# Retention's output projection by seven block products in two phases of two heads, its residual turned by VectorE and its partial sums kept in DRAM

## The chip, the cores and the metric

The kernel runs on one core of a Trainium2 chip. Its time is the device time of one execution in microseconds (us), and the median of several executions is what is compared. The engines of the core are TensorE (PE in the profile; PEld is its loading of weights), VectorE (DVE), ScalarE (ACT), GpSimd (POOL) and SyncE (SP), which here issues most DMAs. Each engine works through its own queue in order.

## The reference

A trunk of two layers on a prompt of 1024 tokens and on 8 single decode tokens, in fp32, with 1024 features. Layer 0 is retention (4 heads, key width 256, value width 512), layer 1 is attention over a sliding window.

```
h = rmsnorm(x, g_norm)
q, k, v, gate = split(h @ w_in)                    # 1024 -> 1024, 1024, 2048, 2048
o, S = retention_scan(q, k, v, S0)                 # in chunks of 128 tokens, head by head
o = rmsnorm(o, g_out) per head                     # over a head's 512 values
o = o * silu(gate)
return x + o @ w_out, S                            # 2048 -> 1024: the projection that changes
```

Layer 1 norms the result, projects it to q, k, v and a gate, attends, and has an output projection and a residual of its own.

## The kernel before

Every fp32 number of a product is split into a high part and a low part (names ending in `_hi`/`h` and `_lo`/`l`), and each product is three matmuls: high by high, low by high, high by low. ACT writes a high part as a copy in PE's format; DVE or POOL subtracts it from the number for the low part.

**Stage 1, retention's input projection (0 to about 532 us).** Mostly by seven block products: tokens are split into even and odd ones, the features in two halves and the output columns in two blocks, so that the product of 2 x 2 by 2 x 2 blocks takes seven block products (table `SEQ7`, L309) of sums of blocks, not eight. The sums of the token side stand in cells (`XH`, `XL`, in two token halves t); those of the weights (S1 to S4) are made set by set. `product` (L312) issues a block product for one token half: 12 matmuls of 128x258 (256 prompt columns and 2 decode columns). `evac` (L361) adds the banks up in SBUF. The order of all other engines is set by a table of planned times: a function is put behind a slot of PE (`later`) or at a planned microsecond (`when`). Gates go through Silu and are stored in DRAM (`gsc`).

**Stage 2, the retention loop (about 532 to 681 us).** 32 steps, a head's chunk each: heads 0 and 1 in turns, then heads 2 and 3. A step has scores and products on PE (`b_qk`, `b_mm`), and behind them the sum of squares (ACT, L987), its power on POOL (L116), the scaling `on` (DVE, L999), a turn by transposes on PE (`b_tr`), and the gated output `og` = turned output x gate (DVE, L1011). Then `b_oh` (ACT, L1018) and `b_ol` (POOL, L1022) split `og` into `A_hi`, `A_lo` (tokens 0 to 511) or `B_hi`, `B_lo` (the rest and the decode tokens). `others(i)` writes each step's operations in a fixed order for every engine.

**Stage 3, the output projection (681 to 878 us).** Plain: for each of 8 blocks of 128 output columns and three groups of tokens (512, 256, 264) 16 contraction tiles x 3 matmuls go into one PSUM bank (`ro_part`, L1214 to L1216). The first of these tiles is woven into the loop's last steps (`b_wmm`, L1055 to L1057). Weights are loaded on SP's queue in tiles of 512 KB and multiplied by the output norm's gain while they are split (L1147, L1148). The residual x_prompt is added by PE: it is transposed into the same bank (`tr`, L101). `ro_finish` copies the sum out (ACT, `x`), splits it times the next norm's gain into `A_hi`, `A_lo` (L1252, L1253), squares it (L1258), adds the squares on POOL (L1259) and stores it to `xscr`; the first token group is read back and split later (`reload2`, L1267, L1268).

**Stage 4** begins with the key and value projection (`kv_mm`, L1387 to L1389), which needs all of `A_hi` and `A_lo`.

## Time and profile before

| | |
|---|---|
| median of 3 runs | 1313.93 us (1312.88 to 1314.59) |
| the profiled execution's own time, its span | 1313.03 us, 1310.9 us |
| PE, DVE, ACT, POOL busy | 98%, 56%, 53%, 48% of the span |
| granted TensorE clock | 0.997 |
| DMA | 193.98 MB, 148 GB/s on average |

A row of a view by stage has the stretch, its length, then for each engine the busy time and the number of instructions, the granted clock, the mean busy share of the 16 DMA engines and the rate. A row of a group has the line, engine and operation, what it writes and reads, the shape, the count, and behind the bars the busy time, the mean duration in ns and the engine's idle time ahead of it, with what ended that. Matmuls are pipelined, so their durations overlap; a matmul's price is the distance between two starts.

### The profile page before, as it was taken

To read this page: it belongs to the slowest core of one execution; us is meant where nothing else is said; L and a number is where in the kernel's file an instruction comes from. 1 tells how busy PE (TensorE), PEld (TensorE's weight loads), DVE (VectorE), ACT (ScalarE), POOL (GpSimd) and SP (SyncE) were. 2 spreads that over 40 slices of the span, in tenths; PEclk is the share of its full clock that TensorE was granted. 3 is DMA by queue.
4 is the path that set the end of the run, shared out by engine and by line. 5 is a ranking of instruction groups with operands and counts; after the bars stand their busy time and mean duration, and the time that the engine had idled before them with its cause. 6 is when DMAs were issued, how large, how long until landed. Compare 5 with 4: busy or idle time off the path is not lost.

```text
span 1310.9 us, 26102 instructions
## 1 busy us (share of the span) xinstructions
PE 1280.8 (98%) x9597; PEld 1208.3 (92%) x9597; DVE 728.0 (56%) x1476; ACT 691.5 (53%) x1722; POOL 630.9 (48%) x800
## 2 busy tenths in 40 slices
PE   6999999999999999999999999999999999999998
PEld 5999999999999999887886889999998999998998
DVE  6944556566565564587784333324565666766321
ACT  5533544554555653577775444445576666666121
POOL 6654534545445544599970110127476676554000
PEclk9999999999999999999999999999999999999999
DMA  6314767677686854456556553452032111237232
GB/s 228 102 61 133 235 200 243 181 234 220 195 241 184 249 172 138 134 177 216 169 163 186 161 166 121 131 147 85 17 100 79 66 59 43 74 109 252 73 96 78
DMA packets 199907, 193.98 MB, mean 148 GB/s; under 512 B 12916, under 2 KB 180140, under 8 KB 199764
## 3 DMA queue, kind: packets, MB, share of 16 engines
q1 hardware_dynamic: 165024, 157.78, 39.4%
q10 hardware_dynamic: 34756, 34.53, 8.3%
q8 instruction: 76, 1.25, 0.4%
q14 instruction: 51, 0.42, 0.1%
HBM read 132.23 MB, written 61.08 MB: 147 GB/s over the span
## 4 chain that ended last, share of the span: by engine, by line
PE 89%; POOL 3%; DVE 2%; DMA 2%; ACT 2%; issue 1%; ACTq 0%; SPq 0%; POOLq 0%; DVEq 0%
PE b L331 7%; PE b L332 7%; PE b L333 7%; PE pj L1167 6%; PE pj L1168 6%; PE pj L1169 6%; PE b L324 4%; PE b L325 4%; PE b L326 4%; PE tr L101 4%; PE pj L1214 4%; PE pj L1216 4%; PE pj L1215 4%; PE o L1645 2%; PE b L538 2%; DMA wr<-in_w_out_ret_dram 1%
## 5 line engine op out<-in xcount | busy, mean ns | idle before, releaser
L331 PE MATMUL b<-xh,woh 128*128 128x258 f32 x784 | 223.2, 285 | 0.0
L333 PE MATMUL b<-xh,wol 128*128 128x258 f32 x784 | 221.7, 283 | 0.0
L332 PE MATMUL b<-xl,woh 128*128 128x258 f32 x784 | 221.6, 283 | 0.0
L1167 PE MATMUL pj<-A_hi,wh 128*128 128x384 f32 (+1 forms) x512 | 174.5, 341 | 2.0 <-ACT A_hi L1665 1.3
L1168 PE MATMUL pj<-A_lo,wh 128*128 128x384 f32 (+1 forms) x512 | 164.7, 322 | 0.2 <-DVE A_lo L1666 0.2
L1169 PE MATMUL pj<-A_hi,wl 128*128 128x384 f32 (+1 forms) x512 | 164.6, 321 | 0.0
L331 PEld LDWEIGHTS b<-xh,woh 128*128 128x128 f32 x784 | 148.0, 189 | 4.1 <-issue 3.7
L332 PEld LDWEIGHTS b<-xl,woh 128*128 128x128 f32 x784 | 148.7, 190 | 0.0
L333 PEld LDWEIGHTS b<-xh,wol 128*128 128x128 f32 x784 | 148.0, 189 | 0.0
L222 POOL TENSOR_TENSOR wol<-raw,woh 128x512 fp32r<-128x512 f32 x52 | 68.1, 1319 | 130.3 <-ACT woh L217 126.2
L324 PE MATMUL b<-woh,xh 128*128 128x256 f32 x448 | 126.6, 283 | 0.0
L325 PE MATMUL b<-wol,xh 128*128 128x256 f32 x448 | 126.0, 281 | 0.0
L326 PE MATMUL b<-woh,xl 128*128 128x256 f32 x448 | 125.6, 280 | 0.0
L1167 PEld LDWEIGHTS pj<-A_hi,wh 128*128 128x128 f32 x512 | 96.8, 189 | 6.0 <-issue 2.6
L1168 PEld LDWEIGHTS pj<-A_lo,wh 128*128 128x128 f32 x512 | 97.1, 190 | 0.4 <-DVE A_lo L1666 0.4
L1169 PEld LDWEIGHTS pj<-A_hi,wl 128*128 128x128 f32 x512 | 96.5, 188 | 0.0
L1148 DVE SCALAR_TENSOR_TENSOR wl<-wr,gcol,wh 128x256 fp32r<-128x256 f32 x128 | 53.9, 487 | 69.9 <-ACT wh L1147 65.8
L1259 POOL TENSOR_TENSOR acc<-acc,sq 128x256 f32<-128x256 f32 (+1 forms) x28 | 20.6, 743 | 148.1 <-ACT sq L1258 148.0
L1625 POOL TENSOR_TENSOR s<-s,sm 128x512 f32<-128x512 f32 x64 | 66.5, 1040 | 47.6 <-DVE sm L1624 43.5
L324 PEld LDWEIGHTS b<-woh,xh 128*128 128x128 f32 x448 | 84.3, 188 | 5.0 <-issue 2.9
L326 PEld LDWEIGHTS b<-woh,xl 128*128 128x128 f32 x448 | 84.3, 188 | 0.0
L325 PEld LDWEIGHTS b<-wol,xh 128*128 128x128 f32 x448 | 84.3, 188 | 0.0
(391 smaller groups left out, 3631.4 us busy)
## 6 DMA issues: line engine op xcount, KB each, us to landing
raw<-in_w_in_ret_dram ACTq DMA_DIRECT2D x44, 512.0 KB
st<-in_state_ret_dram SPq DMA_DIRECT2D x64, 256.0 KB
out_dram<-st SPq DMA_DIRECT2D x64, 256.0 KB
wr<-in_w_out_ret_dram SPq DMA_DIRECT2D x32, 512.0 KB
wr<-in_w_in_swa_dram SPq DMA_DIRECT2D x18, 512.0 KB
vb<-vscr SPq DMA_DIRECT2D x64, 128.0 KB
evp<-qks SPq DMA_DIRECT2D x32, 256.0 KB
evx<-vsc SPq DMA_DIRECT2D x32, 256.0 KB
```

Of the source, the lines that this page charges most:

```text
L222: eng.tensor_tensor(lo, src_of(s, name, sub), hi.bitcast(F32), SUB)
L324: mm(dst, xh, wh, start=a and i == 0, stop=False, skip_group_check=True)
L325: mm(dst, xh, wl, start=False, stop=False, skip_group_check=True)
L326: mm(dst, xl, wh, start=False, stop=z, skip_group_check=True)
L331: mm(dst, wh, xh, start=a, stop=False, **sg)
L332: mm(dst, wh, xl, start=False, stop=False, **sg)
L333: mm(dst, wl, xh, start=False, stop=z, **sg)
L1148: nc.vector.scalar_tensor_tensor(lo[:, k, :], raw[:, k % 4, :], gk, hi.bitcast(F32)[:, k, :], ALU.mult, ALU.subtract)
L1167: mm(ps, hi[:, k, fs], xh[:, k, t0:t1], start=first and k == ks[0], stop=False)
L1168: mm(ps, hi[:, k, fs], xl[:, k, t0:t1], start=False, stop=False)
L1169: mm(ps, lo[:, k, fs], xh[:, k, t0:t1], start=False, stop=last and k == ks[-1])
L1625: nc.gpsimd.tensor_tensor(st[:, :, 0:256], st[:, :, 0:256], sm.unsqueeze(2).broadcast_to([128, 2, 256]), ALU.mult)
```

## The change

Stage 3 is done by stage 1's seven block products. The contraction of 2048 rows is split in two phases: phase 0 has heads 0 and 1, phase 1 heads 2 and 3. Each phase has four sets, one for 256 output columns each; a set's blocks are even and odd tokens, the two heads of the phase, and even and odd output columns. Seven of the eight sets have 7 products x 2 token halves of 12 matmuls 128x258; set 4, the first of phase 1, is computed plainly (8 slots of 24), without sums.

- **Loop.** `on` goes from DVE to ACT; `b_oh` and `b_ol` go away. `og` is stored by a DMA on SP's queue: heads 0 and 1 into cells in SBUF, heads 2 and 3 into DRAM (`osc`). `x_items` makes the token side's sums and splits for phase 0 in the loop, 3 or 4 items a step. The first set's weights are loaded and split there too (`p_early`).
- **Gates.** The output norm's gain is multiplied into the gates in stage 1 (POOL, 64 times 128x258) and no more into the weights.
- **Residual.** `p_xr` loads x_prompt in runs of 64 numbers into one buffer `xr`, half of the tokens at a time; `p_xt` turns it on DVE by 32x32 block transposes (four of 128x256 for a half) into the tiles to which the products are added.
- **Partial sums.** Phase 0's results are stored to DRAM (`pscr`) on ACT's queue and loaded again in phase 1 in place of the residual.
- **Cells of phase 1.** In sets 3 to 5 the gated outputs of heads 2 and 3 are loaded from `osc`, summed and split (`split`, `t_sums`).
- **End.** `p_fin` squares and stores the results; in set 7 it splits them for the next stage, and the six other blocks are read back and split by `a_load` and `a_split`. The key and value projection's weights are loaded and split in set 7. The layout of `xscr` and the order of layer 1's features (even and odd) follow.

```diff
         if s.kind == "g":
             dst, col = gsc, (s.kt + i) % 4
+            pool.tensor_scalar(r[:, 0:258], r[:, 0:258], gcol[:, s.kt + i:s.kt + i + 1], None, MUL)
...
     def b_on(h, c):
         d = heads[h]
-        dve.tensor_scalar(d["on", c], d.pop(("po", c)), d["ss", c], None, MUL)
+        act(d["on", c], d.pop(("po", c)), AF.Copy, scale=d["ss", c])
...
+        o_ = ogt[h % 2]
+        dve.tensor_tensor(o_, d.pop(("pt", c)).rearrange("p (i t) -> p i t", i=4), d["g", c], MUL)
+        nc.sync.dma_start(out=(osc[h - 2, par, t] if h >= 2 else raw_of(((B11, T1), (B21, B22))[h][par], t))[:, :, cs], in_=o_)
...
+        def parts(x, src):
+            n = len(its)
+            do(act, XH[t][x][:, :, cs], src, AF.Copy)
+            do(lambda: (pool if n % 3 else dve).tensor_tensor(XL[t][x][:, :, cs], src, XH[t][x].bitcast(F32)[:, :, cs], SUB))
...
+    def p_bank(i, t):
+        if i < 2:
+            return sSp.tile([128, DV], F32, tag="S", bufs=4, name="S")
+        return pq["b2"].tile([128, 512], F32, tag=f"b2{t}", name="b2")
...
+    def p_evac(s, j, t):
...
+        if j == 0:
+            act(c["p"][:, t], b0, AF.Copy)
+        elif j == 1:
+            dve.tensor_tensor(c["p"][:, t], b1, c["p"][:, t], ADD)
+        elif j == 2:
+            dve.tensor_tensor(c["x"][:, t], b2, c["p"][:, t], ADD)
+        else:
+            key, b = (("c", b0), ("w", b1), ("x", b2), ("p", b1))[j - 3]
+            dve.tensor_tensor(c[key][:, t], b, c[key][:, t], ADD)
...
+    def p_store(s, key):
+        nc.scalar.dma_start(out=pscr[s.a, "cwxp".index(key)].rearrange("p (t n) -> p t n", t=2), in_=s.c[key])
...
+    def p_xr(s, t):
+        v = x_prompt[0, 512 * t:512 * t + 512, 256 * s.a:256 * s.a + 256].rearrange("(n j) (b f) -> b j n f", j=32, b=4)
+        for b in range(4):
+            nc.sync.dma_start(out=pq["xr"][32 * b:32 * b + 32], in_=v[b])
+
+    def p_xt(s, t):
...
+            dve.transpose(o_.rearrange("p (c y) -> p c y", c=2), v[:, par, i])
...
+    def p_fin(s, key, t):
...
+        if s.n == 7:
+            act(toks(A_hi[:, ft], t, par), x1, AF.Copy, scale=gk)
+            dve.scalar_tensor_tensor(toks(A_lo[:, ft], t, par), x1, gk, toks(A_hif[:, ft], t, par), MUL, SUB)
...
+    def t_sums(t, h):
...
+        dve.tensor_tensor(y, hv(raw_of(T1, t), h), b11, SUB)
+        dve.tensor_tensor(z, hv(raw_of(T2, t), h), y, SUB)
+        part(T1, t, h, y, dve)
+        part(T2, t, h, z, pool)
+        dve.tensor_tensor(b11, z, b11, SUB)
+        pool.tensor_tensor(b21, b21, z, SUB)
...
+    def a_split(k):
+        gk = gcol[:, 16 + k:17 + k]
+        lo_ = A_lo[:, k, 0:NP]
+        act(A_hi[:, k, 0:NP], lo_.bitcast(F32), AF.Copy, scale=gk)
+        dve.scalar_tensor_tensor(lo_, lo_.bitcast(F32), gk, A_hif[:, k, 0:NP], MUL, SUB)
...
+            if s.n:
+                for j in range(2):
+                    when(max(s.t0 - 22.0, 1.5) + 0.1 * j, p_raw, s, j)
+            if s.P == 0:
+                a = s.t0 - 9.0 if s.n else 0.5
+                b = s.t0 - 3.0 if s.n else 5.0
+                when(a, p_xr, s, 0)
+                when(b, p_xt, s, 0)
+                when(b + 0.1, p_xr, s, 1)
+                when(b + 5.5, p_xt, s, 1)
+            else:
+                for key in "cwxp":
+                    when(s.t0 - 7.0, p_part, s, key)
...
+            L(n + 13, o_load, raw_of(T1, t)[:, :, 0:256], 0, 1, t)
+            L(m, o_load, raw_of(T2, t)[:, :, 0:256], 1, 1, t)
...
+            for h in range(2):
+                L(m + 2 + 2 * t + h, t_sums, t, h)
...
+        for k in range(6):
+            L(u + 1 + k, a_load, k)
+            L(u + 4 + k, a_split, k)
```

**The loop, on ACT.** This is one step of the loop before (`Sh`: state split, `on,bss`: sum of squares, `vh`, `kh`, `sTh`: splits of values, keys and scores).

```order
L968 ACTIVATE Sh<-S 128x512 x2
L987 ACTIVATE on,bss<-po 128x512
L795 ACTIVATE vh<-evx 128x512
L1018 ACTIVATE B_hi<-og 128x4x128
L770 ACTIVATE kh<-tr,M_85 128x256
L785 ACTIVATE sTh<-sT 128x128
```

And one of the changed kernel's, with an item of `x_items` (L1078).

```order
L1011 ACTIVATE Sh<-S 128x512 x2
L808 ACTIVATE vh<-evx 128x512
L783 ACTIVATE kh<-tr,M_88 128x256
L1042 ACTIVATE on<-po,bss 128x512
L798 ACTIVATE sTh<-sT 128x128
L1078 ACTIVATE SB<-G_7435 128x4x128
L1030 ACTIVATE on,bss<-po 128x512
```

The split of the gated output (L1018) is gone; the scaling `on` (L1042), which reads POOL's `bss`, stands ahead of the split of the scores.

**The turn, on SP.** The changed kernel's queue at the end of the loop: `osc` are the gated outputs, `xr` the residual, `rb` and `ra` weights.

```order
L1056 DMA osc<-og 512x1x128
L747 DMA evw<-gsc 128x512
L1056 DMA osc<-og 512x1x128 x4
L1215 DMA xr<-in_x_prompt_dram 32x16x64 x4
L1131 DMA rb<-in_w_out_ret_dram 128x4x256 x2
L1215 DMA xr<-in_x_prompt_dram 32x16x64 x12
```

The first residual loads stand behind the last steps' stores.

**Set 0, on DVE.** The changed kernel's queue from the last gated output on (`S` and `b` are PSUM banks, `evp`, `evx`, `evc`, `evw` the tiles in which a set is added up, `rx` and `rp` further residual tiles, `w` low parts of weights).

```order
L1055 TENSOR_TENSOR og<-tr,evw 128x512
L1190 TENSOR_TENSOR evp<-S,evp 128x258
L1229 STREAM_TRANSPOSE evw<-xr 128x256
L1229 STREAM_TRANSPOSE evc<-xr 128x256
L1229 STREAM_TRANSPOSE rx<-xr 128x256
L1229 STREAM_TRANSPOSE rp<-xr 128x256
...
L1195 TENSOR_TENSOR evc<-S,evc 128x258
L1229 STREAM_TRANSPOSE evw<-xr 128x256
...
L1229 STREAM_TRANSPOSE rp<-xr 128x256
L1195 TENSOR_TENSOR evc<-S,evc 128x258
```

Evacuations of PSUM banks (L1190, L1195) stand behind turns of the residual, which wait for its loads; before, DVE had only splits of weights and results in this stage.

680 lines of the change are left out of this document (454 added, 226 removed).

## The prediction

> **What bounds the kernel now.** I read the page first, then the busy times by stage, then the stage's groups, PE's waits and the chain.
>
> ```profile
> PE 1280.8 (98%) x9597; PEld 1208.3 (92%) x9597; DVE 728.0 (56%) x1476; ACT 691.5 (53%) x1722; POOL 630.9 (48%) x800
> PE 89%; POOL 3%; DVE 2%; DMA 2%; ACT 2%; issue 1%; ACTq 0%; SPq 0%; POOLq 0%; DVEq 0%
> ...
> core 0: us, PE busy (x) PEld busy (x) DVE busy (x) ACT busy (x) POOL busy (x), PEclk, DMA share, GB/s
> 340.00:505.00 165.00, 165.00 (x1390) 161.18 (x1389) 98.41 (x174) 89.74 (x204) 73.83 (x96) 1.00 0.69 204
> 618.00:672.00 54.00, 54.00 (x297) 45.86 (x296) 42.37 (x97) 38.59 (x92) 49.60 (x59) 1.00 0.55 175
> 700.00:718.00 18.00, 15.97 (x66) 11.31 (x66) 9.07 (x21) 11.39 (x30) 1.43 (x2) 1.00 0.77 234
> 718.00:798.00 80.00, 80.00 (x435) 68.31 (x435) 25.79 (x62) 35.09 (x92) 8.74 (x12) 1.00 0.46 143
> ```
>
> PE is busy 98% of the span and makes 89% of the chain, at full granted clock. In the output projection (718 to 798) the three other engines are at 11 to 44%, so a product less there is time less, until the new work fills them. In the loop ahead of it (618 to 672) POOL is at 92% and DVE at 78%: little room. The projection runs from its first product to the first of the key and value projection:
>
> ```profile
> 681.47 0.47 PE L1055 MATMUL S<-A_hi,woh 128*128 128x512 f32 x1
> 877.71 0.36 PE L1387 MATMUL pj<-wh,A_hi 128*128 128x256 f32 x1
> ...
> L1214 PE MATMUL pj<-A_hi,wh 128*128 128x512 f32 x112 | 45.1, 403 | 2.4 <-ACT wh L1147 2.4
> L1214 PE MATMUL pj<-B_hi,wh 128*128 128x264 f32 x128 | 37.0, 289 | 0.0
> L1214 PE MATMUL pj<-B_hi,wh 128*128 128x256 f32 x128 | 36.8, 287 | 0.0
> L101 PE MATMUL pj<-ident,xr 128*128 128x128 f32 x60 | 10.7, 280 | 0.0
> ```
>
> That is 196.2 us. The durations in groups overlap (pipelined), so a product's price is read from start to start:
>
> ```profile
> 734.09 0.39 PE L1214 MATMUL pj<-A_hi,wh 128*128 128x512 f32 x1
> 739.84 0.40 PE L1215 MATMUL pj<-A_lo,wh 128*128 128x512 f32 x1
> ...
> 479.89 0.28 PE L331 MATMUL b<-xh,woh 128*128 128x258 f32 x1
> 492.75 0.28 PE L333 MATMUL b<-xh,wol 128*128 128x258 f32 x1
> ```
>
> 25 steps in 5.75 us make 0.230 us for 512 columns; 107 steps in 12.86 us make 0.1202 us for 258 columns, the first stage's form and the one that the change uses.
>
> **What goes from PE.** The new stage has seven sets of 7 products x 2 token halves x 12 matmuls and one plain set of 8 x 24, 1368 matmuls of 258 columns: 164.4 us. A slot of 12 is 1.44 us, a set 20.2, the plain one 23.1. Gain: 196.2 - 164.4 = 31.8 us. The residual's PE transposes and PE's 2.4 us of waits on weights are inside the 196.2. Everything below is what eats into it.
>
> ```profile
> L222 DVE TENSOR_TENSOR wol<-s,woh 128x512 fp32r<-128x512 f32 x88 | 67.5, 770 | 11.1 <-ACT woh L217 11.0
> L376 DVE TENSOR_TENSOR evp<-b,evp 128x258 f32<-128x258 f32 x26 | 11.1, 426 | 13.3 <-PE b L333 13.3
> L999 DVE TENSOR_SCALAR on<-po,bss 128x512 f32<-128x512 f32 x31 | 23.3, 750 | 14.0 <-POOL bss L116 14.0
> L1022 POOL TENSOR_TENSOR A_lo<-og,A_hi 128x512 fp32r<-128x512 f32 x16 | 20.7, 1292 | 0.0
> L1018 ACT ACTIVATE A_hi<-og 128x512 fp32r<-128x512 f32 x16 | 10.2, 637 | 0.4 <-DVE og L1011 0.4
> L1589 POOL TENSOR_SCALAR ndp<-C 128x256 f32<-128x256 f32 x16 | 13.7, 854 | 13.8 <-DVE s L1613 12.8
> ```
>
> **Gates in the first stage.** 64 new scalings on POOL x 0.854 = 55 us, by the row of 256 columns. From 340 to 505 POOL has 91 of 165 us free, and what waits behind a scaling is one store and the release of its buffer. Lower bound 0, upper 5 (should one POOL burst hold a set's buffers); I take 1.0.
>
> **The loop.** Over 32 steps POOL loses b_ol (32 x 1.29 = 41 us) and gains 18 low parts (23 us). ACT loses b_oh (20 us), gains `on` (32 x about 0.6) and 28 high parts (18 us). DVE loses `on` (24 us) and gains 16 sums and 10 low parts at 0.77 (20 us) with 14 pairs of decode columns. So the totals nearly cancel; the order does not. The 14.0 us that DVE waited for POOL's power go over to ACT, where the score split sTh and the state split Sh stand behind `on`, and PE's next products wait for both. ACT had 15.4 of 54 us free. Each og also becomes a DMA on SP's queue, ahead of the next steps' q, k, v and gate loads; those are issued two steps ahead, which covers it. POOL, the fullest engine, gets lighter, so a gain of 2 us is possible; the other bound is +10 (most of the 14 us exposed). I take +2.5.
>
> **The turn.**
>
> ```profile
> 684.82 0.75 DVE L999 TENSOR_SCALAR on<-po,bss 128x512 f32<-128x512 f32 x1 [0.72 <-POOL bss L116]
> 687.75 0.69 DVE L1011 TENSOR_TENSOR og<-tr,evw 128x512 f32<-128x512 f32 x1 [0.47 <-PE tr L101]
> ...
> 674.36 3.05 DMA evx<-in_w_out_ret_dram
> 704.42 5.29 DMA wr<-in_w_out_ret_dram
> 697.60 4.54 DMA wr<-in_w_out_ret_dram
> ...
> 797.32 0.37 SPq L1226 DMA_DIRECT2D xr<-in_x_prompt_dram  x1
> L806 DVE CAST qh<-evp 128x256 fp32r<-128x256 f32 x28 | 9.6, 341 | 0.0
> ```
>
> The last norm ended 4.1 us after the stage's first product. In the new order its turn on PE stands behind two slots (2.9 us): PE waits 1.2 us (0 to 3). Then come the turn (0.6) and og (0.7), so the last og is ready 5.4 us after the stage's first product, and only behind its store, on SP's queue, stand the four residual loads of set 0's first token half.
>
> **Set 0's residual.** One half is 512 KB in 2048 runs of 256 bytes. 256 KB in 512-byte runs landed in 3.05 us, 512 KB in 1 KB runs in 4.54: 1.56 fixed and 1.49 for each 512 runs of 512 bytes. By bytes a half lands in 4.5 us; if a run of 256 bytes is as dear as one of 512, in 1.56 + 4 x 1.49 = 7.5, and with four issues of 0.37 in 9.0. I take 5.5, near the bytes, since the queues are otherwise nearly empty at that point. Four turns of 128x256 on DVE cost 1.4 (the cast of that size) to 3.1 (0.77 each); I take 1.6. There is one landing buffer: the second half's loads wait for the first half's turns. So the second half is turned at 5.4 + 2 x 7.1 = 19.6, and behind it in DVE's queue stands the evacuation of the fourth product's second half (0.4), which frees the PSUM bank that the ninth slot after the first, at 9 x 1.44 = 13.0, writes. PE waits 7.0 us; bounds 17.6 - 13.0 = 4.6 and 30.0 - 13.0 = 17.0.
>
> The Trainium skill (DMA: Bandwidth & Descriptors, Specifications) speaks against these loads: under 512 bytes a transfer does a read-modify-write and falls from line rate. No run here shows such loads; by it a half lies at its upper bound, 9.0, and the sum comes out as in the slower rival.
>
> The later sets of phase 0 start their first half 9 us ahead. A cycle of two halves is 14.2 of 20.2 us, covered by the set before; stores of the partial sums run on ACT's queue. I take 1.0; with 12.1 a half, 3 x (24.2 - 20.2) = 12.
>
> **Sets 3 to 5, where the cells are made again.** Twelve reloads of 512 KB of gated outputs, 1 MB of partial sums and 1 MB of weights: 8 MB, at the 234 GB/s of 700 to 718 some 36 us, where set 3 and the plain set last 43.3. The last sums need T2, which lands last, and behind it DVE does four times two sums, a low part and one more sum (4 x 4 x 0.77 = 12.3), evacuations (8 x 0.43), two more low parts, decode columns and the low part of set 5's first operand, in all about 27 us in the plain set's 23.1. Counted by DVE alone set 5 starts 4 us late; counted from the landing of T2, with half of the sums behind it and the rest of the queue, 36 + 12.3 + 10 - 43.3 = 15. I take 7.0: T1 lands earlier, so part of the sums is done by then. Set 6: 0.5 (0 to 2).
>
> **Set 7 and the tail.**
>
> ```profile
> L1268 DVE SCALAR_TENSOR_TENSOR A_lo<-wr,gcol,A_hi 128x512 fp32r<-128x512 f32 x8 | 6.0, 752 | 9.8 <-ACT A_hi L1267 9.8
> L1267 ACT ACTIVATE A_hi<-wr,gcol 128x512 fp32r<-128x512 f32 x8 | 5.8, 722 | 7.9 <-DMA wr<-xscr 7.9
> L1253 DVE SCALAR_TENSOR_TENSOR A_lo<-pj,gcol,A_hi 128x256 fp32r<-128x256 f32 x8 | 3.9, 483 | 24.1 <-ACT A_hi L1252 23.8
> L1252 ACT ACTIVATE A_hi<-pj,gcol 128x256 fp32r<-128x256 f32 x8 | 3.7, 467 | 0.0
> L1258 ACT ACTIVATE sq<-x 128x256 f32<-128x256 f32 x21 | 8.5, 413 | 0.3
> ```
>
> In the last ten slots (14.4 us) ACT has six splits of 1024 columns (6 x 1.44) and eight A_hi and squares (8 x 0.88): 15.7 us; DVE has 6 x 1.50 + 8 x 0.48 + 8 x 0.43 and the decode columns, about 17.5. Before, nearly all of that lay under PE. The next projection needs every A_lo: 3 us late, and the last evacuation, split and square follow the last product. I take 4.0 (2 to 8).
>
> **Costed at nothing.** The norm gains' new order (two transposes on PE early in the first stage), the decode columns' small stores, and the next projections' weights loaded in pairs of rows (runs of 1 KB as before) lie under DMA engines that are half idle here; a weight load without that cover would cost its landing, up to 5.3 us.
>
> **The sum.** 1.0 + 2.5 + 1.2 + 7.0 + 1.0 + 7.0 + 0.5 + 4.0 = 24.2 against 31.8: 7.6 us less than the profiled execution's 1313.0, so 1305.4. The median of the runs is 0.9 above that execution: 1306.
>
> **The rivals.** (1) The bounds' lower ends hold: -2 + 4.6 + 4 + 2 = 8.6 of losses, 1291. For it: other engines at 11 to 44% in this stage. Against it: single buffers and in-order queues. 0.18. (2) ACT paces the loop: its new wait for POOL's power is exposed, +10 in place of +2.5, 1314, no change. For it: those 14.0 us, and that PE is never idle there now. Against it: 28% of ACT is free. 0.14. (3) Slower: the residual's loads pace phase 0. If loading and turning a half costs 12.1 us in place of 7.1, set 0 loses 17 and each later set of the phase 4: 21 us more than in the sum, 1327. From 10.1 us a half (half of a set) it decides every set. For it: 256-byte runs that no row shows, one buffer, and DVE's queue in which evacuations stand behind the turns. (The Trainium skill's rule named above would act through this rival.) Against it: DMA engines at half load. With sets 3 to 5 near 15, lesser cases of it also end slower. 0.25. My forecast has 0.43, with 1300 to 1312 as its own range.
>
> What differs by under 0.2% (2.6 us) cannot be told from no change. Of my 0.43 some 0.03 falls there, with rival 2 it is 0.17; faster 0.40 + 0.18 = 0.58; slower 0.25. The range 1291 to 1324 reaches to rivals 1 and 3.
>
> **What would show it.** Products at 0.120 us and set 1 in 20 to 21 us bear out the gain. PE waiting on an evacuation (L1195) near the tenth slot, with DVE waiting for xr, shows set 0's term and its size; the same in sets 1 to 3 is rival 3. Set 5's start behind DVE's L1166 or L1331 shows that term; steps over 4.7 us with PE waiting for sTh or Sh are rival 2. I am wrong if PE waits under 10 us in all, or if it waits most where the three other engines are idle.

## The result and the profile after

The changed kernel is slower: 1359.7 us (1358.83 to 1364.17, 4 runs) against 1314.26 us (1312.88 to 1314.77, 4 runs) of the kernel before on the same chip, a ratio of 1.0354 (95% interval 1.0330 to 1.0378). Forecast was 1306 us.

The head of the profile's page and its chain of waits by engine, of the kernel after:

```profile
span 1357.0 us, 26895 instructions
PE 1277.7 (94%) x9743; PEld 1216.5 (90%) x9743; DVE 822.9 (61%) x1590; ACT 693.6 (51%) x1664; POOL 812.6 (60%) x994
PE 70%; DVE 8%; POOL 7%; ACT 5%; issue 5%; DMA 4%; SPq 1%; ACTq 0%; DVEq 0%; POOLq 0%
```

The span grew by 46.1 us (1357.0 against 1310.9). PE's share of the chain fell from 89% to 70%. POOL's work grew by 182 us (812.6 against 630.9) and DVE's by 95. The next view is PE's timeline after: the first product of each of the eight sets, and the first of the key and value projection. The columns are start, duration, line, what is written and read, shape and count.

```profile
537.14 0.47 PE L991 MATMUL S<-first 128*128 128x512 f32 x1 [0.61 <-DVE raw L379]
...
702.49 0.36 PE L334 MATMUL S<-SA,EO 128*128 128x258 f32 x1
731.64 0.28 PE L334 MATMUL S<-SA,w 128*128 128x258 f32 x1
752.09 0.28 PE L334 MATMUL S<-SA,w 128*128 128x258 f32 x1
772.29 0.28 PE L334 MATMUL S<-SA,w 128*128 128x258 f32 x1
799.40 2.82 PE L1289 MATMUL S<-SA,w 128*128 128x258 f32 x22
828.35 0.58 PE L334 MATMUL S<-SA,w 128*128 128x258 f32 x1 [5.58 <-ACT w L1161]
861.98 0.28 PE L334 MATMUL S<-SA,w 128*128 128x258 f32 x1
882.18 0.28 PE L334 MATMUL S<-SA,w 128*128 128x258 f32 x1
...
917.26 0.55 PE L1710 MATMUL pj<-kv,SA 128*128 128x256 f32 x1 [1.12 <-DVE evx L1195]
```

The first row starts the loop; the same instruction before started at 536.62. Taken from start to start, and with the sum's own figures for the sets (20.2 us for 168 matmuls, 23.1 for the plain 192), the 46 us lie so:

| stretch | before | after | forecast of the difference |
|---|---|---|---|
| stage 1, to the loop's first product | 536.6 | 537.1 (+0.5) | +1.0 |
| loop, to the projection's first product | 144.9 | 165.35 (+20.5) | +2.5 |
| projection | 196.2 | 214.8 (+18.5) | -31.8 + 20.7 |
| of it: matmuls alone | | 164.4 (-31.8) | -31.8 |
| set 0 (29.15 against 20.2) | | +8.95 | +8.2 (turn and residual) |
| sets 1 and 2 | | +0.2 | +1.0 |
| sets 3 to 5 (89.7 against 63.5) | | +26.2 | +7.0 |
| set 6 | | 0 | +0.5 |
| set 7 and tail (35.1 against 20.2) | | +14.9 | +4.0 |
| behind the projection, to PE's last instruction | 429.5 | 436.1 (+6.5) | 0 |

Set 6 runs at 20.2 us and sets 1 and 2 nearly so: the seven products cost what was worked out. What they wait for in the other sets is in the list of PE's waits after (line of PE, what it waited for, then us in all, times, longest):

```profile
PE tr L104 <- ACT on L1042: 20.7, 19, 2.9
PE S L336 <- DVE w L1166: 10.7, 3, 5.2
PE S L334 <- DVE evw L1195: 8.2, 4, 6.0
...
PE S L336 <- POOL w L1166: 6.7, 4, 2.3
PE S L334 <- ACT w L1161: 5.6, 1, 5.6
```

The first row is the loop, but for one wait of 2.1 us in set 0: 18 turns that came late, 18.6 us. In all, PE's idle time in the loop grew from 5.7 to 19.1 us; of the other 7 us of the loop's loss some 3 are a stretch of half clock from 673 to 680 (explained below), and the rest is spread over single steps. The rows of `w` (L1161 writes the high part of a set's weights, L1166 the low part) and of `evw` are the sets. PE's waits before had one large row in these stages, 4.9 us for `on`.

Busy times by stretch after (the columns are those of this view before):

```profile
620.00:650.00 30.00, 25.85 (x140) 20.70 (x139) 27.03 (x62) 23.03 (x54) 21.64 (x26) 1.00 0.83 267
740.00:760.00 20.00, 20.00 (x166) 19.79 (x166) 13.29 (x28) 4.97 (x9) 13.22 (x16) 1.00 0.61 167
820.00:840.00 20.00, 9.23 (x51) 8.72 (x51) 18.55 (x29) 8.30 (x17) 13.70 (x14) 0.67 0.45 136
900.00:920.00 20.00, 12.37 (x69) 11.63 (x68) 12.35 (x20) 9.45 (x19) 12.02 (x21) 0.72 0.22 66
```

In these 30 us of the loop DVE is now the fullest engine (27.03), where POOL was before (49.60 of 54). Over the whole loop no engine is: DVE is busy for 120.5 of 165.35 us, ACT for 121.0, POOL for 123.6, where before it was 110.1, 105.7 and 127.7 of 144.85. In set 1 (740 to 760) PE has no gap. Around the start of set 5 (820 to 840) DVE is busy 93% of the time and PE 46%. The granted clock, 1.00 in every stretch of this stage before, is 0.67 there and 0.72 around the end of set 7.

**Half clock.** PE's timeline after, at set 5:

```profile
834.34 0.58 PE L336 MATMUL S<-SA,w 128*128 128x258 f32 x1 [5.19 <-DVE w L1166]
834.72 0.42 PE L334 MATMUL S<-SA,w 128*128 128x258 f32 x1
834.94 0.42 PE L335 MATMUL S<-SA,w 128*128 128x258 f32 x1
```

Behind a wait of 5.2 us the products step by 0.22 us (834.72, 834.94; 0.215 on average), not by 0.120. The clock had been at half since 826.84, when PE stood in the wait of 5.6 us ahead of that one, and stayed there for 13.65 us. Another such stretch begins at 908.76 in a wait of 6.0 us. Four more in the projection last 3.4 us; they begin within or just behind waits of 3.8 us (to 788.1), of 2.3 (to 893.6), of 1.0 and 2.0 (to 855.4 and 857.9), and of 0.8 and 1.4 (to 725.5 and 727.4). Counted from all starts in the projection, 119 steps are slow and cost 11.2 us more than at full clock. So of the projection's 50 us of losses 11 are the clock and some 39 are left for the waits themselves.

**DVE and POOL take turns.** The timelines of DVE and then of POOL after, in the same 10 us (L1331 to L1335 and L1336 are the sums of sets 3 to 5, L1321 their low parts, L969 and L970 the decode columns):

```profile
821.92 0.69 DVE L1332 TENSOR_TENSOR xr<-SA,xr 128x512 f32<-128x512 f32 x1
...
824.08 1.33 DVE L1331 TENSOR_TENSOR s2a<-SA,G 128x512 f32<-128x512 f32 x1
825.52 1.57 DVE L1332 TENSOR_TENSOR s1a<-SA,s2a 128x512 f32<-128x512 f32 x1
827.01 1.99 DVE L1321 TENSOR_TENSOR SA<-s2a,SA 128x512 fp32r<-128x512 f32 x1
...
829.52 0.41 DVE L1295 TENSOR_TENSOR evx<-S,evx 128x258 f32<-128x258 f32 x1
...
830.69 1.18 DVE L970 TENSOR_TENSOR SA<-dT,SA 128x8 fp32r<-128x8 f32 x1
...
833.51 0.17 DVE L970 TENSOR_TENSOR SA<-dT,SA 128x8 fp32r<-128x8 f32 x1
```

```profile
823.36 1.50 POOL L1321 TENSOR_TENSOR SA<-xr,SA 128x512 fp32r<-128x512 f32 x1 [1.48 <-ACT SA L1320]
824.83 1.71 POOL L1336 TENSOR_TENSOR G<-G,xr 128x512 f32<-128x512 f32 x1
826.50 1.95 POOL L1145 TENSOR_TENSOR s1b<-rb 128x512 f32<-128x512 f32 x1
...
829.00 1.63 POOL L1321 TENSOR_TENSOR SA<-s1a,SA 128x512 fp32r<-128x512 f32 x1
830.59 1.26 POOL L1336 TENSOR_TENSOR G<-G,s1a 128x512 f32<-128x512 f32 x1
```

At 821.92, with POOL idle (its operation at 823.36 had waited 1.48 us), DVE's sum of 128x512 takes 0.69 us. The three that begin while POOL works end 0.5 to 0.6 us after POOL's operation: 824.08 + 1.33 = 825.41, and POOL's first ended at 824.86; 825.52 + 1.57 = 827.09 after 826.54; 827.01 + 1.99 = 829.00 after 828.45. So each waited for POOL's operation to end and then took its 0.6 us. POOL's next operations are longer by about as much: 1.71 and 1.95 where DVE stood in between, 1.26 at 830.59 beside 8-column operations only. A decode column pair's subtraction takes 0.17 us alone and 1.18 beside POOL. The evacuation at 829.52, which reads PSUM, takes 0.41 us beside POOL's low part (829.00) as elsewhere. From 700 to 920 DVE has 64 operations on 128x512 with two operands in SBUF. The 24 that meet no two-operand operation of POOL take 0.68 us, the 40 that meet one 1.13 on average. Of these 40, 27 take longer than 0.7 us. Each of the 27 began while POOL's operation was under way, and 26 of them end 0.54 to 0.56 us after it ended. A large DVE operation and a large POOL operation together cost about 1.9 us (0.6 + 1.26), not the longer of the two.

The Trainium skill says so (SBUF — State Buffer, "SBUF: two separate sides"): VectorE and GpSimd share one pair of ports as an exclusive lock, held for a whole instruction, and a VectorE operation with two SBUF inputs needs it against a GpSimd operation that reads SBUF. The durations above agree.

**Set 0.** The chain of waits after, at set 0's residual (start, duration; a load's from its issue to its landing, here the last of the four loads of a half):

```profile
711.55 4.90 DMA xr<-in_x_prompt_dram
716.95 0.40 DVE evc L1229
719.47 3.64 DMA xr<-in_x_prompt_dram
723.30 0.46 DVE evw L1229
```

The first half's loads are issued from 709.81 on and are in 6.6 us later (711.55 + 4.90 = 716.45), the second half's from 718.03 on and in 5.1 us later (723.11); 5.5 was forecast for both. A turn takes 0.40 to 0.46 us; 0.4 was forecast. In this set PE waits 2.1 us for the last step's `on`, 1.7 for a low part of the weights behind the first half's turns, 0.8 for an evacuation behind the second half's, and 1.4 for a low part on POOL behind that; the half clock costs 2.0 more.

### The profile page after: what moved, and what is told of

Read it like the earlier page. It is cut to its first block, busy times and chain, and to the rows that moved or that the text cites. A ratio compares the mean times of both kernels' runs of the same rounds, so it can differ in the third digit from the quotient of the medians.

```text
span 1357.0 us, 26895 instructions
## 1 busy us (share of the span) xinstructions
PE 1277.7 (94%) x9743; PEld 1216.5 (90%) x9743; DVE 822.9 (61%) x1590; ACT 693.6 (51%) x1664; POOL 812.6 (60%) x994
## 3 DMA queue, kind: packets, MB, share of 16 engines
q8 instruction: 77, 1.26, 0.4%
## 4 chain that ended last, share of the span: by engine, by line
PE 70%; DVE 8%; POOL 7%; ACT 5%; issue 5%; DMA 4%; SPq 1%; ACTq 0%; DVEq 0%; POOLq 0%
PE b L334 7%; PE b L335 7%; PE b L336 7%; PE pj L1607 5%; PE pj L1608 5%; PE pj L1609 5%; PE b L327 4%; PE b L328 4%; PE b L329 4%; PE tr L104 3%; PE b L543 2%; PE S L336 2%; PE S L334 1%; PE S L335 1%; PE o L1970 1%
## 5 line engine op out<-in xcount | busy, mean ns | idle before, releaser
L1607 PE MATMUL pj<-SA,wh 128*128 128x384 f32 (+1 forms) x512 | 174.7, 341 | 2.3 <-ACT SA L1990 1.3
L1608 PE MATMUL pj<-SA,wh 128*128 128x384 f32 (+1 forms) x512 | 164.3, 321 | 0.2 <-DVE SA L1991 0.2
L1609 PE MATMUL pj<-SA,wl 128*128 128x384 f32 (+1 forms) x512 | 164.5, 321 | 0.0
L1607 PEld LDWEIGHTS pj<-SA,wh 128*128 128x128 f32 x512 | 96.7, 189 | 6.5 <-issue 2.6
L1608 PEld LDWEIGHTS pj<-SA,wh 128*128 128x128 f32 x512 | 96.9, 189 | 0.4 <-DVE SA L1991 0.4
L1609 PEld LDWEIGHTS pj<-SA,wl 128*128 128x128 f32 x512 | 96.5, 188 | 0.0
L1940 ACT ACTIVATE s<-s,mx 128x257 f32<-128x257 f32 x128 | 64.2, 505 | 38.2 <-DVE mx L1938 37.3
L220 ACT ACTIVATE woh<-s 128x512 fp32r<-128x512 f32 x88 | 54.1, 624 | 53.3 <-POOL s L210 20.6
```

The costliest lines, as they stand in the source:

```text
L1607: mm(ps, hi[:, k, fs], xh[:, k, t0:t1], start=first and k == ks[0], stop=False)
L1608: mm(ps, hi[:, k, fs], xl[:, k, t0:t1], start=False, stop=False)
L1609: mm(ps, lo[:, k, fs], xh[:, k, t0:t1], start=False, stop=last and k == ks[-1])
L1940: nc.scalar.activation(st[:, j, :], st[:, j, :], AF.Exp, bias=mx[:, j:j + 1], accum_out=sm[:, j:j + 1])
```

## The experiments

Three losses were to be explained: the loop (20.5 us), sets 3 to 5 (26.2) and set 7 (14.9). Each time below is that of one profiled execution, except in the last two experiments, which are timed against the kernel before. In the changed kernel and three variants that leave the loop as it is, the loop's stretch came out at 165.35, 167.6, 166.55 and 166.9 us; differences below 2.3 us are not read.

### The loop: scaling back on DVE

PE's largest wait is for `on` on ACT, the engine that the rival of an ACT-paced loop names. This run moves it back.

```diff
-        act(d["on", c], d.pop(("po", c)), AF.Copy, scale=d["ss", c])
+        dve.tensor_scalar(d["on", c], d.pop(("po", c)), d["ss", c], None, MUL)
```

> One part undone: the scaling `on` of the loop goes back from ScalarE to VectorE, at the same place of the program. The stretch from the loop's first product to the projection's first product is 144.9 us before and 165.4 us with the change. Theory A (`on` holds up ScalarE's queue while it waits for GpSimd's power, and the score and state splits stand behind it): at most 150 us. Theory B (the sums and splits that the change puts into the loop fill VectorE and GpSimd, and make their operations longer where both read SBUF): 160 us or more, since VectorE gets 24 us more. Theory C (the stores of the gated outputs on SyncE's queue hold up the loads behind them): unchanged, 163 to 168 us.

Measured: loop 167.0 us, no change; the run 1365.2 us. PE now waits for DVE's `on`, 20.1 us in 17 waits. That ACT is what holds the loop up is out: the name of the engine in the wait list moved with the instruction, the wait did not go.

### The loop: without the sums and splits

```diff
-            items += x_items((i - 5) // 8, (i - 5) // 4 % 2)
+            if (i - 5) // 4 % 2 == 0:
+                for x in range(7):
+                    t_z = (i - 5) // 8
+                    items.append(lambda c=XH[t_z][x]: pool.memset(c.bitcast(F32), 0.0))
...
```

> The sums and splits of phase 0's token side are left out of the loop; in their place GpSimd sets the same cells to zero, so phase 0's products are of zeros. `on` stays on ScalarE and the stores stay on SyncE's queue. The loop's stretch is 165.4 us with the change and 144.9 us before. Theory B: at most 150 us, and VectorE's and GpSimd's operations on SBUF go back to their durations of before (the query split's low part on GpSimd 743 ns, now 855). Theory A: 160 us or more, with PE waiting for `on`. Theory C: 158 us or more, with the value loads landing late as now.

Measured: loop 149.1 us, 16.3 less; 1340.13 us for the run. PE's wait in the loop:

```profile
PE tr L104 <- ACT on L1042: 6.1, 5, 2.4
```

Sets 0 and 1 lose 5.45 us together in place of 9.2, with the same residual loads. So the loop's leftover items cost some 4 us behind it, too. The remaining 4.2 us of the loop (149.1 against 144.9) have other causes, which no run tells apart.

### The loop: the store of og one step later

The rival for the loop's loss was SP's queue, where each `og` now is a transfer ahead of the next loads. Here each store is issued a step later, behind those loads.

```diff
-        nc.sync.dma_start(out=(osc[h - 2, par, t] if h >= 2 else raw_of(((B11, T1), (B21, B22))[h][par], t))[:, :, cs], in_=o_)
+        o_st.append((dst, o_))
...
+        o_flush(1 if i < NS - 1 else 0)
```

> The stores of the gated outputs are issued one step later on SyncE's queue, behind the next step's loads of queries, values and gates, so that the queue never stands at a store whose gated output isn't ready. Theory C: the loop's stretch falls from 165.4 us to 155 or less and ScalarE's wait for the values (4.7 us) goes away. Theories A and B: 162 us or more.

Measured: loop 183.3 us, 17.9 more. DVE's waits in the loop have a new first row (`og` writes into one of two tiles, and waits for the tile's last store):

```profile
DVE og L1055 <- DMA SA<-og: 15.5, 8, 6.6
```

The delay of the stores came back as a wait of DVE, because a gated output's buffer is free only once it is stored. ACT's wait for the values, which the queue's order could explain, was 4.7 us in the changed kernel's loop (540 to 695): too little for 20 us; here it is 2.0. The theory of SP's queue falls, although this run is a poor test of it, since it put another wait in its place.

### The loop: the low parts on one engine

The changed kernel has 18 low parts on POOL and 10 on DVE. All on POOL (shown), and likewise all on DVE:

```diff
-            do(lambda: (pool if n % 3 else dve).tensor_tensor(XL[t][x][:, :, cs], src, XH[t][x].bitcast(F32)[:, :, cs], SUB))
+            do(lambda: pool.tensor_tensor(XL[t][x][:, :, cs], src, XH[t][x].bitcast(F32)[:, :, cs], SUB))
```

> All 28 low parts of phase 0's cells are made by GpSimd in the loop (now 18 of them, VectorE 10). The loop's stretch is 165.4 us with the change, 149.1 with no such work at all, 144.9 before. If VectorE's amount of work is what makes the loop long: 158 us or less. If the two engines' holding each other up on SBUF is: 164 us or more, and VectorE's sums in the loop at 1.2 us or more (now 1.07 on the mean).

> All 28 low parts of phase 0's cells are made by VectorE in the loop, none by GpSimd. Holding each other up on SBUF: GpSimd has 23 us less, so fewer of VectorE's operations are stretched and the stretch of the loop is at most 160 us. VectorE's amount of work: 168 us or more, since VectorE gets 18 operations of 0.7 to 1.2 us more.

Measured: 166.2 us with all on POOL, 170.0 with all on DVE; the runs 1359.62 and 1363.65 us. The first is no change. The second is 3.4 above the mean of the unchanged loops, and in neither way does the loop get shorter. Neither theory comes out whole. With all on POOL the loop stays as long as the holding up on SBUF would have it, but VectorE's sums take 1.02 us on the mean, where that theory had 1.2 or more. With all on DVE the loop is as long as VectorE's amount of work would have it, and the other theory's 160 us or less are missed. So it stays open how much of the loop's loss is DVE's amount of work and how much the holding up.

### The loop: ACT's part alone, and ACT's and POOL's

Two runs put the loop together step by step. In the first, of the items only ACT's high parts stay. It also loads the first half of set 0's residual in the loop and gives the second half a buffer of its own, and puts set 7's splits three slots later. In the second, ACT's high parts and 28 low parts on POOL stay; besides, POOL's operations on the cells of sets 3 to 5 are put on DVE.

```diff
-        do(dve.tensor_tensor, tm[0], r[T1], r[B11], SUB)
-        do(dve.tensor_tensor, tm[1], r[B22], tm[0], SUB)
-        parts(T1, tm[0])
...
+        for x in (T2, T3, T4):
+            parts(x)
...
-            L(u + 4 + k, a_split, k)
+            L(u + 7 + k, a_split, k)
```

> Three stages, one edit each. Loop: of phase 0's sums and splits only ScalarE's 28 high parts stay, at their places; VectorE's and GpSimd's are left out (GpSimd sets to zero what nothing writes), so phase 0's products are wrong. The loop's stretch is 165.4 us with the change, 149.1 with none of the work. Theory J (ScalarE's copies stand in its queue ahead of the state splits and of `on`, and that is what PE waits for): 158 us or more. Theory K (VectorE's and GpSimd's part): 152 us or less. Set 0: the residual of its first token half is loaded during the loop, into the tile of the sums of squares, which is free then; the second half has the landing buffer from the start. If the chain load, turn, load, turn is what PE waits for there, set 0 takes at most 25 us in place of 29.2; if not, 27 or more. Set 7: the six splits of the blocks that are read back are put three slots later, behind more of the evacuations. If their place in the queue is what counts, set 7 takes at most 30 us in place of 35.1; if their amount is, 33 or more.

> Loop: ScalarE's 28 high parts and 28 low parts, all on GpSimd, stay; VectorE's sums and decode columns are left out, so phase 0 is wrong. With everything and all low parts on GpSimd the loop's stretch was 166.2 us. If VectorE's sums are the larger part of the loss: 156 us or less. If GpSimd's low parts are: 162 us or more. Sets 3 to 5: all of the cells' making that GpSimd had is done by VectorE. With the change these sets lose 26.2 us; with GpSimd's part left out 10.3. If the two engines' holding each other up on SBUF is the larger part of the difference: at most 20 us, although VectorE gets 20 operations of 0.7 us more. If the amount of work is: 26 us or more.

Measured loops: 149.5 us with ACT's part, 152.6 with ACT's and POOL's. With what stands above, this is a ladder: 149.1 without items, 149.5 with 28 high parts, 152.6 with 28 low parts on POOL as well, 166.2 with DVE's 16 sums and 14 pairs of decode columns on top (the run with all low parts on POOL). DVE's step costs 13.6 us. By durations before, 16 sums at 0.77 are 12.3; in the changed kernel's loop they are dearer. Its groups (line, engine, shape, count, then busy us and mean ns, idle time ahead):

```profile
L1078 DVE TENSOR_TENSOR G<-G,SA 128x512 f32<-128x512 f32 x4 | 5.2, 1300 | 0.0
L1078 DVE TENSOR_TENSOR G<-SA,G 128x512 f32<-128x512 f32 x4 | 4.7, 1173 | 0.0
L1078 DVE TENSOR_TENSOR G<-SB,G 128x512 f32<-128x512 f32 x4 | 4.4, 1107 | 0.1
L1078 DVE TENSOR_TENSOR G<-SA 128x512 f32<-128x512 f32 x4 | 2.8, 702 | 5.9 <-POOL SB L1083 5.9
```

Three of the four groups take 1.1 to 1.3 us; the one that stands behind an operation of POOL that it needs, and waited for it in two cases, 0.70. Together 17.1 us. How the 13.6 us divide between the sums and the decode columns was not tried alone. The run with plain sets below has 16 high parts, 16 low parts on POOL and 8 pairs of decode columns in the loop, but no sums, and its loop takes 147.9 us; that speaks for the sums.

Set 0: with ACT's part alone and the residual early, sets 0 and 1 lose 2.45 us together (22.65 and 20.2). Against the run without items (5.45) the early residual is worth 3.0 us. Set 7: 36.0 us in the first of these runs, with splits three slots later, against 35.1. So a place three slots further back gains nothing.

Sets 3 to 5 in the second run: 25.6, 29.95 and 30.5 us, together 22.6 above the matmuls, against 26.2. A move of POOL's operations to DVE gains 3.6 us of 26. That lies between what the two theories said (at most 20, or 26 or more) and decides for neither; in the eight kernels that leave these sets alone they take 89.4 to 91.9 us, so the gain is 3 to 6 us. The next runs bear on this.

### Sets 3 to 5: without the cells, and without POOL's part

In the first run the sums, splits and decode columns of phase 1's cells are left out, and the loads stay. In the second only POOL's operations of that work are.

```diff
     def split(x, t, src=None, engs=None, y=None):
-        for h in range(2):
-            part(x, t, h, hv(raw_of(x, t) if src is None else src, h), (engs or (dve, pool))[h])
-        dec_cols(pq["dT"], 8, x, t, y)
+        return
...
     def t_sums(t, h):
-        y, z = [v.rearrange("p (k n) -> p k n", k=2) for v in pq["yz"][h]]
+        return
```

```diff
         act(hi, src, AF.Copy)
-        eng.tensor_tensor(lo, src, hi.bitcast(F32), SUB)
+        if eng is dve:
+            eng.tensor_tensor(lo, src, hi.bitcast(F32), SUB)
...
-        pool.tensor_tensor(b21, b21, z, SUB)
```

> In sets 3 to 5 the sums and splits of phase 1's token side are left out (ScalarE, VectorE, GpSimd); the loads of the gated outputs stay, and phase 1 multiplies phase 0's cells. The seven-product sets take 20.2 us and the plain one 23.1 us where nothing waits; with the change set 3 takes 27.1, the plain set 28.9, set 5 33.6: 26.2 us too much. Theory D (this work overfills VectorE's queue): the three sets together lose at most 5 us, and the projection takes 190 us in place of 214.8. Theory E (the reloads and SyncE's queue are what is late): they lose 15 us or more as now. If the stalls go, the half granted clock behind them goes too, and with it some 4 us of the loss.

> In sets 3 to 5 GpSimd's part of the cells' making is left out (the low parts of half of the contraction tiles and one sum), VectorE's and ScalarE's part and all loads stay; phase 1's sums are wrong by that. Sets 3, plain and 5 take 27.1, 28.9 and 33.6 us with the change, 26.2 us over 20.2, 23.1, 20.2; without any cell making they lost 0.1 us. VectorE's additions of two SBUF operands of 128x512 took 0.68 us there where GpSimd was not in a two-operand operation and 1.19 where it was. Theory F (the two engines hold each other up on SBUF): these operations go back to 0.7 and the sets' loss falls to 6 to 14 us. Theory G (VectorE has too much of its own to do in any case): 18 us or more stay.

The first products of sets 3 and 6, of the run without cells and then of the run without POOL's part:

```profile
775.09 0.28 PE L334 MATMUL S<-SA,w 128*128 128x258 f32 x1
...
838.69 0.28 PE L334 MATMUL S<-SA,w 128*128 128x258 f32 x1
```

```profile
773.90 0.28 PE L334 MATMUL S<-SA,w 128*128 128x258 f32 x1
...
847.65 0.28 PE L334 MATMUL S<-SA,w 128*128 128x258 f32 x1
```

Without cells the three sets take 63.6 us, where their matmuls alone are 63.5: all of the 26.2 us goes with the making of the cells, and the 8 MB of transfers, from which the forecast had worked out its upper bound, cost nothing as traffic. What their landing times cost this run can't show, since nothing in it reads what they bring. In the changed kernel ACT stands idle for the first of them, 6.0 us until 781.8:

```profile
L1320 ACT ACTIVATE SA<-G 128x512 fp32r<-128x512 f32 x8 | 4.6, 621 | 9.2 <-DMA G<-osc 6.0 <-DVE evc L1195 3.2
```

DVE, idle for 3.2 us, starts its low part behind it, and PE waits 3.8 us for DVE until 788.09, in set 3. Without POOL's part ACT waits there too (5.5 us), and the three sets take 73.75 us, set 3 23.0 of them: 16 of the 26 us go with POOL's 16 low parts and 4 sums. The runs took 1334.93 and 1347.05 us.

Put beside the run that gives POOL's part to DVE (3.6 us gained), this fits two engines that take turns: the work costs nearly the same on either, and only less of it is shorter. The fit is an argument from three runs and the two timelines; a run in which DVE's operations read PSUM, which would take the turns away alone, was not made.

### Set 7: without reading back and splitting

```diff
         for k in range(6):
-            L(u + 1 + k, a_load, k)
-            L(u + 4 + k, a_split, k)
+            pass
```

> In set 7 the reading back and splitting of the six blocks of layer 1's input is left out; the next projection then multiplies what stands in those places. Set 7 takes 35.1 us with the change, 20.2 where nothing waits. Theory H (the splits stand in VectorE's queue ahead of the evacuations, and wait there for the loads): set 7 takes at most 24 us. Theory I (the chain of a result of the last set, out of the bank, split, squared, is what holds PE): 28 us or more.

PE's timeline, the first product of set 7 and the first of the next projection:

```profile
881.87 0.28 PE L334 MATMUL S<-SA,w 128*128 128x258 f32 x1
...
906.88 0.39 PE L1709 MATMUL pj<-kv,SA 128*128 128x256 f32 x1
```

25.0 us in place of 35.1: the six blocks cost 10.1 of the 14.9 us (the run: 1349.15 us). That is just above the 24 us of theory H and well under the 28 of theory I; the other 4.8 us were not taken apart. In the changed kernel DVE's part of the blocks, and two rows of DVE's timeline there:

```profile
L1345 DVE SCALAR_TENSOR_TENSOR SA<-SA,gcol 128x1024 fp32r<-128x1024 f32 x6 | 9.9, 1648 | 6.7 <-ACT SA L1344 6.7
...
907.06 2.20 DVE L1345 SCALAR_TENSOR_TENSOR SA<-SA,gcol 128x1024 fp32r<-128x1024 f32 x1 [0.86 <-ACT SA L1344]
909.18 0.41 DVE L1195 TENSOR_TENSOR evw<-S,evw 128x258 f32<-128x258 f32 x1
```

9.9 us of DVE at 1.65 each, close to the 1.50 of the forecast, but with 6.7 us of idle time ahead, when DVE's queue stood at a split whose high part ACT hadn't written (4.3 of them ahead of the first split). Evacuations and the next low parts of weights stood behind it: for the evacuation at 909.18 PE waited 6.0 us.

### All eight sets plain

What is left of the change if it makes no sums: all sets have 8 products. The cells are the gated outputs themselves, `on` is on DVE, and set 0's residual comes early as above.

```diff
-        s.n, s.P, s.a, s.kind, s.fw, s.plain = n, n // 4, n % 4, "p", 128, n == 4
+        s.n, s.P, s.a, s.kind, s.fw, s.plain = n, n // 4, n % 4, "p", 128, True
...
-        do(dve.tensor_tensor, tm[0], r[T1], r[B11], SUB)
...
+        for x in (B11, T3, B21, B22):
+            do(act, XH[t][x][:, :, cs], src, AF.Copy)
+            do(pool.tensor_tensor, XL[t][x][:, :, cs], src, XH[t][x].bitcast(F32)[:, :, cs], SUB)
...
```

> What is left of the change when the block products are taken out of it: all eight sets are computed plainly (8 slots of 24 matmuls, 1536 in all, 184.6 us by 0.1202 each, where the projection took 196.2 before and the change's products 164.4), so no sums are made in the loop or in sets 3 to 5. The residual is still turned by VectorE, set 0's first half is loaded during the loop, `on` is on VectorE again, the partial sums still go over DRAM, heads 2 and 3 are split during phase 0, and four blocks in place of six are read back in set 7. If the work beside the products is what the change fails on, the loop's stretch is 145 to 151 us (165.4 with the change), sets 0 to 6 take 23.1 to 25 us each, set 7 at most 30, and the whole time is within 10 us of the kernel before on either side. If the phases, the stores and the residual by VectorE cost much by themselves, it stays over 1330 us.

Measured: 1313.35 us (10 runs) against 1310.57 (13 runs), a ratio of 1.0022 (1.0013 to 1.0032). Loop 147.9 us, projection 187.0, the rest 435.5. The loop, the sets and the whole time are all within what was expected if the work beside the products is what the change fails on. The view by stretches:

```profile
720.00:780.00 60.00, 60.00 (x499) 60.00 (x499) 25.05 (x64) 10.52 (x18) 7.57 (x13) 1.00 0.57 163
```

PE has no gap in 60 us, at full clock, with DVE at 42% and POOL at 13%. The projection is 9.2 us shorter than before without a single block product saved: 8 x 23.1 = 184.8 us of matmuls of 258 columns, without the residual's transposes. The loop (+3.0) and what follows the projection (+6.0) give that back. So one part of the forecast's gain, some 11 of the 31.8 us, is not the seven products at all but the form, and as built here the form costs 9 us elsewhere; the other 20 us (7 sets x 2.9) are what the sums were made for.

### The sums in phase 0

The last attempt at those 20 us: phase 0 and set 7 plain, sets 4 to 6 by products, their sums made during sets 1 to 3 where DVE and POOL are idle by the rows above. In set 7 of this kernel two blocks of layer 1's input are written over a cell that the set still multiplies, so its result is wrong, and nothing is concluded from set 7 or from the time of the whole.

```diff
-        s.n, s.P, s.a, s.kind, s.fw, s.plain = n, n // 4, n % 4, "p", 128, n == 4
+        s.n, s.P, s.a, s.kind, s.fw, s.plain = n, n // 4, n % 4, "p", 128, n < 4 or n == 7
...
-            L(n + 13, o_load, raw_of(T1, t)[:, :, 0:256], 0, 1, t)
+            L(n1 + 1, o_load, raw_of(T1, t)[:, :, 0:256], 0, 1, t)
...
-                L(m + 2 + 2 * t + h, t_sums, t, h)
+                L(n1 + 6 + 4 * t + 2 * h, t_sums, t, h)
...
```

> As the plain sets' kernel, but three sets (4, 5, 6) use the block products again, and the token side's sums for them are made during sets 1 to 3, where that kernel left VectorE, GpSimd and ScalarE busy for 42%, 13% and 18% of 720 to 780 us; what is left of the cells' making for set 4 is splits without sums. Set 7 is plain, from a cell loaded again. Products: 5 x 23.1 + 3 x 20.2 = 176.1 us against 184.6. If the block products were worth their arithmetic and only the place of the side work was wrong, sets 0 to 6 wait for at most 4 us in all, the projection takes 178 to 183 us, and the whole is 3 to 8 us shorter than with plain sets, so the same as the kernel before or up to 0.4% faster. If the weights' sums, the evacuations and the splits of set 4 alone fill VectorE, sets 3 to 5 lose 8 us or more and the gain is gone.

Measured: 1334.38 us (5 runs) against 1311.62 (9 runs), a ratio of 1.0169 (1.0150 to 1.0188). The four plain sets of phase 0 take 101.6 us where they took 94.4 in the kernel with plain sets only; the 7 us are set 2's (30.4 in place of 23.2). Set 4 takes 32.6 in place of 20.2, sets 5 and 6 20.6 and 20.7. The making of the cells costs 7 us in phase 0, where the sums are, and 12 in set 4, where splits without sums are left, with three sets of products to earn 9. The expectation that this work finds room there falls.

## Why the prediction was wrong

**Right: the gain.** 0.1202 us a product, 164.4 us of matmuls: sets 2 and 6 take 20.2 us, and without cells the plain one 23.2. The forecast's first sign of being right, set 1 in 20 to 21 us, held (20.45).

**Right in size, in part by luck: gates and set 0.** Gates cost 0.5 us (1.0 forecast). The turn and set 0's residual were put at 8.2 us, and the set lost 8.95; a half landed in 6.6 and 5.1 us. Rival 3, the residual as the pace of phase 0, is out: sets 1 and 2 lose 0.2. The cause of set 0's loss was only partly the named one: 7.0 us were to be a wait for one evacuation behind the second half's turns, and PE waited 0.8 us there; the turn, waits for low parts of weights and the half clock made up the rest. The early residual won back 3.0 us, and the loop's leftover items some 4.

The Trainium skill's rule on short runs (DMA: Bandwidth & Descriptors, Specifications) would have had the half at its upper bound of 9.0 us. 512 KB in runs of 256 bytes landed in 4.90 and 3.64 us from the last issue, about as fast as 4.54 us for 512 KB in runs of 1 KB; the trace does not agree, and the measurement decides.

**Wrong: the loop, "+2.5" where it was +20.5.** The step that failed is "So the totals nearly cancel". It added up durations by engine: DVE loses `on` (24 us), gains sums and low parts at 0.77. The totals of DVE did not cancel: over the loop its work rose from 110.1 to 120.5 us. `on` went (23.3 us), and there came 17.1 us of sums, since most take 1.1 to 1.3 us with POOL at work, 7.5 of low parts, 0.73 to 1.2 each, and 8.2 of decode columns, which the forecast named and gave no price. 0.77 was itself a mean: of a line (L222) whose instances take 0.68 us where they meet no operation of POOL, and 0.88 where they do. That DVE still has 45 us free in the loop says that its total is not the whole of it; its order of work may count too, and no run takes the two apart. The rival of an ACT-paced loop had PE wait for the splits of scores and state behind `on`. PE waited for `on` itself, whichever engine had it; by the ladder of runs DVE's sums and decode columns, 13.6 us, are the larger part of the cause.

**Wrong: sets 3 to 5, "I take 7.0" where it was 26.2.** Two bounds were counted, 4 by DVE's operations and 15 by loads. As traffic the loads cost nothing, and all 26 go with the operations on the cells, one late landing among what they wait for. The step that failed is to count by DVE alone: "in all about 27 us in the plain set's 23.1". It left POOL's 20 operations on the cells out. Where the two take turns, their times add up: 16 us of the 26 go with POOL's part.

**Wrong: set 7, "I take 4.0" where it was 14.9.** ACT's 15.7 us and DVE's 17.5 us of work for 14.4 us of slots were about right by size (DVE's splits 1.65 each in place of 1.50). The step that failed is to lay the two side by side: each split is first ACT's and then DVE's, and in DVE's queue evacuations stand behind a split that waits (6.7 us). The six blocks cost 10.1; moved three slots on they cost no less.

**Left out: the clock.** Every wait was priced at its length. In the projection 11.2 us more came from half clock, in stretches of 3.4 and 13.65 us at waits of 0.8 to 6.0 us. The Trainium skill has this rule (TensorE: Matmul & The Clock Gate, "HAM oscillation — how this bites in real kernels"): idle gaps of PE over some 3.4 us bring the clock down to half. The waits of 3.8 to 6.0 us agree, each with a half clock at it and steps of 0.22 behind; but half clock also came at waits of 2.3 us and less, which the rule does not have, and there the trace decides. The profile before showed granted clock 1.00 in every row of this stage, and the forecast kept it for a stage in which PE would wait.

**Left out: what follows, +6.5.** It was costed at nothing. By the wait lists from 917 on, PE waits 8.8 us where it waited 4.8 before (the norm's squares 3.5 against 2.3, a wait of 1.7 us for `kkl` that is new, 0.8 for the scores), and the half clock of set 7's end reaches 5.1 us into it; the slow stretches there cost 4.1 us in all, where they cost 3.2 before. Some 1.6 us are in neither. The run with plain sets has +6.0 there, so most of it doesn't come from the sums. No run takes it apart; it stays open.

In sum: loop 18.0, sets 3 to 5 19.2, set 7 10.9 and the rest 6.5 us above their terms, 54.6, with -1.0 in the small terms: 53.6 us between 1305.4 and the profiled run's 1358.8 (53.4).

## What to carry to other kernels

A saving on the bound engine is worth what the other engines can pay for it in that stretch: here the sums that save 20 us of products, with their splits, cost 16 us in the loop, 4 behind it and 26 in sets 3 to 5. Before pricing added VectorE or GpSimd work by a mean of the trace, look at which of its instances ran beside the other engine, and where both have two-operand work on SBUF, add their times instead of laying one under the other. And before choosing the algorithm that saves products, measure the plain one in the same form: its projection had 9 of the 32 us without any of the sums, and the loop and what follows gave the 9 back.

## What the runs showed of the hardware that was not expected

- DVE's and POOL's operations on two SBUF operands exclude each other for a whole instruction each: 0.69 us alone, up to 1.99 behind POOL; an operation of 8 columns goes from 0.17 to 1.18, and a cast of 8 columns, with one SBUF operand, from 0.16 to as much as 1.28. DVE's 32x32 block transposes of 128x256 (0.40 to 0.46) and its evacuations out of PSUM (0.38 to 0.43) take the same beside POOL as without it.
- Short waits of PE are dearer than their length: a wait of 5.2 us was followed by products at 0.215 us in place of 0.120, and the slow stretches come in lengths of 3.4 and 13.65 us in the projection and 6.8 in the loop.
- Loads in runs of 256 bytes were about as fast as those in runs of 1 KB: 512 KB in 3.64 to 5.75 us from the last issue, over the six halves that DVE waited for, beside 4.54 us.
